# Key weights' low halves on VectorE, the first norm's spread one hook later, and a third in-projection block issued in two halves in a long convolution's last quarter

## The chip, the cores and the metric

The kernel runs on one core of one Trainium2 chip. The metric is the device time of one execution in microseconds (us). The engines are named as the profile names them: PE is TensorE (matrix products), PEld its weight load, DVE is VectorE, ACT is ScalarE, POOL is GpSimd and SP is the engine that issues the DMAs.

## What is computed

Two consecutive layers of a diffusion backbone work on 512 latent tokens of width 1024, with 256 context tokens. Layer 0 mixes with multi-head latent attention, layer 1 with an order-2 Hyena mixer; a gated feed-forward network with a three-tap convolution follows each. The two places that matter here, cut from the reference:

```python
hx = modulate(rmsnorm(x, norm_mix_g[i]), sh1, sc1)      # before each mixer
kv = h @ w_dkv                                          # layer 0, keys and values

def hyena_mixer(u, w_in, b_in, ...):                    # layer 1
    z = dwconv3(u @ w_in + b_in, conv_w, conv_b)
    x1, x2, v = jnp.split(z, 3, axis=-1)
    h_fwd, h_bwd = hyena_filters(...)
    v = v * x2
    y = (two_sided_fftconv(v, h_fwd, h_bwd) + v * d_bias) * x1
    return y @ w_out + b_out
```

`rmsnorm` needs the reciprocal root of the mean square of each token. `two_sided_fftconv` is a convolution over all 512 tokens, done in the kernel by matrix products with DFT tables.

## The kernel before

**Precision.** Nearly every matrix product is made of three: each operand is split into a high half (a rounded copy) and a low half (the rest), and `mm3` issues high x high, high x low and low x high into one accumulator. The names end in h and l: `wh`, `wl` are a weight tile's halves, made by `split_w` (lines 152 to 162) from the loaded `wr`: ScalarE casts `wh` (L158), and VectorE, or whichever engine is passed as `sub`, subtracts to get `wl` (L159), in columns of 1024.

**The start.** `filter_phase` computes the Hyena filters' spectra (`fps`, `fa`, `fb`, `fo` on TensorE; `fev` L503/504 and `fs` L514 on VectorE, stored to DRAM). In its gaps it calls `between()`, which each time runs the next entry of a list, the hooks: modulation rows, the squares of the first norm, then `nm.roots` (the reciprocal roots by three Newton rounds of L336 to L338, tile `rsq` of 128x128), then `spread`. `spread` calls `nm.finish`: VectorE writes `sqd` (L353), and TensorE's product with a matrix of ones, `bc`, spreads the roots over the partitions. Behind it, two hooks add the squares of the context (`add_ctx`: ScalarE squares at L312, GpSimd adds at L314, the last square is VectorE's at L319). Hooks HK (6) and 7 also load and split the key weights `wdkv0` (2048 columns) and `wdkv1` (1024 columns), with `sub` on GpSimd. Then `latents` forms the modulated input on VectorE and ScalarE (`hx` L365, `hxh` L366, `hxl` L367), and `kv` is its first product.

**The long convolution.** `hyena` works in four quarters of 256 channels, each a generator, `quarter(qi)`. A quarter projects three blocks of 256 columns: block 0 and 1 (`in_gemm`, accumulators `hz`) give the factors whose product is `u`; block 2 gives the gate `x1`, needed only at the very end of the quarter. `conv(b)` applies the three taps (L376 to L378, then the edge columns L1119/L1120). `turn` transposes u (`pt` on TensorE) into `uh`, `ul`. The forward DFT (`ua`, `ub`) follows, and the spectrum's steps: `se` (ScalarE) and `eo` (VectorE), then for each of two `kt`: sums `s`, products with the filter `fq` (`m`: half on VectorE, half on GpSimd), `zs`, `se`, and the split into `zzeh`, `zzel`, `zzoh`, `zzol` (cast on ScalarE at L1225, difference on VectorE at L1226). The inverse DFT, `py`, uses them; `yf` (L1239) is py times the gate. The quarters are interleaved by the loop at the end of `hyena`: while one quarter projects, the one before it finishes. In the last quarter nothing follows but the output projection (`project`, accumulators `pj`, weights `wout`), which needs `yh` and `yl`, the halves of yf. `split_y(range(6))` makes the first six chunks (ScalarE L1245, VectorE L1246), `split_y(range(6, 8))` the last two. yh and yl lie in the same memory as hh and hl, the input of the in-projection.

**What sets the order.** The program is written as one stream of calls; a scheduler lays it out into one queue for each engine, and an instruction may move ahead of others that it does not depend on. Each queue then runs strictly in its order. TensorE's accumulators, and the tiles with one or two buffers, tie the engines together.

Of the kernel before, what the change touches and what calls it, by code (L numbers as in the profile page):

```python
# [17 lines left out]
P = 128  # L18
# [8 lines left out]
HK = 6  # L27
# [31 lines left out]
def hybrid_kernel(ctx, tc, A, out):  # L59
    nc = tc.nc  # L60
# [463 lines left out]
    def mla():  # L524
        L = {}
        with ExitStack() as st:
            a1 = st.enter_context(tc.tile_pool(name="a1", bufs=1, side="left"))
            x = a1.tile([P, NC, T], F32, tag="x", name="x")
            xc = a1.tile([P, NC, TC], F32, tag="xc", name="xc")
            s2 = pick[1] = a1.tile([P, 8, 32], F32, name="s2")  # L530
            nc.gpsimd.memset(s2, 0.0)
            act(out=s2[:, :, 0], in_=V("c"), func=AF.Silu)
            act(out=s2[:, :, 1], in_=V("cctx"), func=AF.Silu)
            nc.gpsimd.tensor_copy(out=sc, in_=s2[:, :, 0])
            make_pick(a1)
            psum_pool(st, "pa", 5)
            mods = Mods([(0, 0, 2), (0, 2, 2)])

            slots = [(wp, "wh", 2), (wp, "wh", 2), (wp, "wl", 2), (wp, "wl", 2), (a1, "mw", 2), (a1, "mw", 2),
                     (wp, "wr", 3), (wp, "wr", 3)]  # L540
            ws = []

            def early():
                ws.extend(mods.load(mods.todo[k], *slots[k]) for k in range(NE))

            def ahead():
                ws.extend(mods.load(mods.todo[k], a1, "mw", 2) for k in range(2))

            def first_loads():
                ws.extend(mods.load(mods.todo[k], *slots[k]) for k in range(NE, 4))  # L550
                for i in range(4):
                    dma(out=x[:, 2 * i:2 * i + 2, :], in_=A["x"][:, 2 * i:2 * i + 2, :])
                ws.extend(mods.load(mods.todo[k], *slots[k]) for k in range(4, 8))
                dma(out=xc, in_=A["ctx"])

            nm = Norm(NC, 4, D, a1)
            nm_ctx = []
            hooks, started, wk = [], [], []
            L["wdkv"] = wk

            def between():
                if not started:
                    started.append(True)
                    first_loads()
                    step = lambda: mods.step_pe(1, ws, a1)
                    add = lambda j: (lambda: nm.add(x[:, j, :]))

                    def add_ctx(j0):
                        if not j0:
                            nm_ctx.append(Norm(NC, 2, D, a1))  # L570
                        for j in range(j0, j0 + 4):
                            nm_ctx[0].add(xc[:, j, :])

                    hooks.extend([()] * 2 + [(step, add(0), add(1))] + [(step, add(j)) for j in range(2, 8)] + [(step, ahead)])
                    hooks.append((lambda: L.update(yx=nm.roots(0, None, lane["last"])),))

                    def spread():
                        L["bcx"] = pso("bc")
                        nm.finish([L["bcx"]], 0, None, lane["last"], L["yx"])

                    hooks.append((spread,))
                    hooks.extend((lambda j=j: add_ctx(j),) for j in (0, 4))
                    hooks[HK] += (lambda: wk.append(split_w(A["wdkv0"], 2048, nc.gpsimd.tensor_tensor)),)
                    hooks[7] += (lambda: wk.append(split_w(A["wdkv1"], 1024, nc.gpsimd.tensor_tensor)),)
                elif hooks:
                    for f in hooks.pop(0):
                        f()

            filter_phase(early, between, mods)
            while hooks:  # L590
                between()
            at = atx.enter_context(tc.tile_pool(name="at", bufs=1, side="right", reuse_waits="tile"))
            L["at"] = at
            L["cos"] = at.tile([P, T], F32, name="cosq")
            L["sin"] = at.tile([P, T], F32, name="sinq")
            L["ckh"] = at.tile([P, 2, TK], F32R, name="ckh")
            L["ckl"] = at.tile([P, 2, TK], F32R, name="ckl")
            L["kb"] = [(at.tile([P, TK], F32R, name=f"kh{i}"), at.tile([P, TK], F32R, name=f"kl{i}")) for i in range(2)]
            dma(out=L["cos"], in_=A["rope"][0])
            dma(out=L["sin"], in_=A["rope"][1])  # L600
            with tc.tile_pool(name="a2", bufs=1, side="left", reuse_waits="tile") as a2:
                latents(lambda n: mods.step_pe(n, ws, a1, 2), nm, nm_ctx[0], a1, a1, a2, x, xc, L)
        with ExitStack() as st:
            ab = st.enter_context(tc.tile_pool(name="ab", bufs=1, side="left", reuse_waits="tile"))
            psum_pool(st, "pb", 7, 1)
            return attention(ab, L)
# [497 lines left out]
    def hyena(hh, hl):  # L1104
        with tc.tile_pool(name="hy", bufs=1, side="left", reuse_waits="tile") as hy:
# [17 lines left out]
            def quarter(qi):  # L1123
# [5 lines left out]
                x1 = []  # L1129
                pss = {}  # L1130

                def in_gemm(bs, parts):
# [5 lines left out]
                        jobs += [(pss[b][0], *w, 0), (pss[b][1], *w, P)]  # L1138
                    gemm(jobs, lambda k: hh[:, k, :], lambda k: hl[:, k, :], 8, parts)

                us = {}
                dv = lambda t: t.rearrange("p (n two) -> p two n", two=2)
                dv4 = lambda t: t.rearrange("p (n four) -> p four n", four=4)
# [28 lines left out]
                conv(1)  # L1172
                yield
                turn(0)
                in_gemm((2,), (slice(None),))
                conv(2)
                turn(1)
                yield
                if not M:
# [9 lines left out]
                for o in range(2):  # L1189
                    pa, pb = two((pst if o else pso)("ua")), two((pst if o else pso)("ub"))  # L1190
                    for i, ps in enumerate((pa, pb)):
                        for ci in range(2):
                            mm3(ps[:, ci], M[o][0][:, 2 * i + ci, :], M[o][1][:, 2 * i + ci, :], uh[:, 2 * i + o, :],
                                ul[:, 2 * i + o, :], True, True)
                    e = hy.tile([P, 2, 256], F32, tag="se", name="se", bufs=1)
                    nc.scalar.copy(out=e, in_=pa)
                    s0 = hy.tile([P, 2, 256], F32, tag=f"eo0{o}", name="eo0", bufs=1)
                    s1 = hy.tile([P, 2, 256], F32, tag=f"eo1{o}", name="eo1", bufs=1)
                    vtt(out=s0, in0=e, in1=pb, op=ALU.add)
                    if o:  # L1200
                        for ci in range(2):
                            vtt(out=s1[:, 1 - ci], in0=e[:, ci], in1=pb[:, ci], op=ALU.subtract)
                    else:
                        vtt(out=s1[:, 0], in0=e[:, 0], in1=pb[:, 0], op=ALU.subtract)
                        vtt(out=s1[:, 1], in0=pb[:, 1], in1=e[:, 1], op=ALU.subtract)
                    eo.append((s0, s1))
                for kt in range(2):
                    zs = []
                    for si, op in enumerate((ALU.add, ALU.subtract)):
                        s = eo[1][kt] if si else hy.tile([P, 2, 256], F32, tag="s0", name="s0", bufs=1)  # L1210
                        vtt(out=s, in0=eo[0][kt], in1=eo[1][kt], op=op)  # L1211
                        f = fq[:, kt, si]
                        m1 = hy.tile([P, 2, 256], F32, tag="m1", name="m1", bufs=1)
                        vtt(out=m1, in0=s, in1=f, op=ALU.mult)  # L1214
                        z = hy.tile([P, 2, 256], F32, tag=f"zs{si}", name=f"zs{si}", bufs=1)
                        vtt(out=z[:, 0], in0=m1[:, 0], in1=m1[:, 1], op=ALU.subtract)
                        m2 = hy.tile([P, 2, 256], F32, tag="m2", name="m2", bufs=1)
                        nc.gpsimd.tensor_tensor(out=m2[:, 0], in0=s[:, 0], in1=f[:, 1], op=ALU.mult)  # L1218
                        nc.gpsimd.tensor_tensor(out=m2[:, 1], in0=s[:, 1], in1=f[:, 0], op=ALU.mult)
                        nc.gpsimd.tensor_tensor(out=z[:, 1], in0=m2[:, 0], in1=m2[:, 1], op=ALU.add)  # L1220
                        zs.append(z)
                    for nm, op in (("e", ALU.add), ("o", ALU.subtract)):
                        s = hy.tile([P, 2, 256], F32, tag="s0", name="se", bufs=1) if nm == "e" else zs[1]
                        vtt(out=s, in0=zs[0], in1=zs[1], op=op)
                        nc.scalar.copy(out=zz[nm + "h"][:, kt], in_=s)  # L1225
                        vtt(out=zz[nm + "l"][:, kt], in0=s, in1=zz[nm + "h"][:, kt], op=ALU.subtract)  # L1226
# [210 lines left out]
```

## Time and profile before

| | |
|---|---|
| median of 3 runs | 1436.95 us (1435.52 to 1437.35) |
| profiled execution | 1438.24 us |
| its span | 1436.5 us |
| mean granted TensorE clock | 0.987 of full speed |
| PE busy | 1368.1 us (95%) |
| DVE busy | 965.6 us (67%) |
| ACT busy | 563.8 us (39%) |
| POOL busy | 238.9 us (17%) |

The profile is of one execution. Its span is the time from the first to the last instruction; the execution's own time is 1.7 us longer. Times in the rows below are from the span's start. A busy share is an average over stages that are limited by different things, so the rows below are read stage by stage.

### The profile page before, as it was taken

How to read it: one execution, taken by the hardware profiler on the slowest of the kernel's cores; microseconds unless marked ns; L12 is line 12 of the kernel's file. 1: busy time of each engine (PE TensorE's matmuls, PEld its weight loads, DVE VectorE, ACT ScalarE, POOL GpSimd, SP SyncE). 2: the span in 40 equal slices, each digit the busy share in tenths (PEclk: the TensorE clock that was granted, in tenths of full speed). 3: DMA queues.
4: the chain of work that ended last, by engine and by line, in shares of the span. 5: the costliest groups of instructions: out<-in, count | busy, mean ns of one | idle time of the engine just before them, and what ended most of it. 6: DMA issues, size and time to landing. Idle time of an engine off the chain costs nothing. (4 is left out here: it accounts for less than half of the span.)

```text
span 1436.5 us, 17449 instructions
## 1 busy us (share of the span) xinstructions
PE 1368.1 (95%) x6774; PEld 1073.1 (75%) x6774; DVE 965.6 (67%) x1473; ACT 563.8 (39%) x859; POOL 238.9 (17%) x216
## 2 busy tenths in 40 slices
PE   6789899999999999999999999999999999999996
PEld 3467666665589788787878988787788888888886
DVE  5766767677359777567764788988786553455545
ACT  5434455556335343134442443232344431234330
POOL 4701046456220000000001011332300000000011
PEclk9999999999999999999999999999999999999998
DMA  9663522224233645655514342222313213322121
GB/s 365 241 236 123 142 70 79 73 78 166 71 129 123 229 160 200 245 204 178 183 61 143 123 162 89 92 85 89 121 62 112 93 68 119 117 89 79 61 81 59
DMA packets 47966, 186.58 MB, mean 130 GB/s; under 512 B 5464, under 2 KB 18136, under 8 KB 33676
## 3 DMA queue, kind: packets, MB, share of 16 engines
q1 hardware_dynamic: 47884, 185.48, 37.2%
q8 instruction: 53, 0.87, 0.2%
q14 instruction: 29, 0.24, 0.1%
HBM read 171.29 MB, written 11.60 MB: 127 GB/s over the span
## 5 line engine op out<-in xcount | busy, mean ns | idle before, releaser
L158 ACT CAST wh<-wr 128x1024 fp32r<-128x1024 f32 (+1 forms) x203 | 190.2, 958 | 181.0 <-PE dn L69 89.3
L159 DVE TENSOR_TENSOR wl<-wr,wh 128x1024 fp32r<-128x1024 f32 x200 | 233.4, 1183 | 12.2 <-ACT wh L158 9.5
L314 POOL TENSOR_TENSOR sqa<-sqa,sq 128x512 f32<-128x512 f32 (+1 forms) x42 | 51.6, 1229 | 830.7 <-ACT sq L312 775.4
L69 PE MATMUL dn<-gh,wl 128*128 128x512 f32 (+1 forms) x396 | 147.0, 371 | 0.0
L69 PE MATMUL dn<-gh,wh 128*128 128x512 f32 (+1 forms) x396 | 146.6, 371 | 0.0
L69 PE MATMUL dn<-gl,wh 128*128 128x512 f32 (+1 forms) x396 | 146.6, 370 | 0.0
L377 DVE SCALAR_TENSOR_TENSOR z<-ua,vec,z 128x511 f32<-128x511 f32 x44 | 33.0, 749 | 107.1 <-ACT z L376 107.1
L1096 DVE SCALAR_TENSOR_TENSOR x<-dn,modc,x 128x512 f32<-128x512 f32 (+1 forms) x36 | 24.9, 691 | 108.8 <-PE dn L69 108.8
L376 ACT ACTIVATE z<-ua,vec 128x512 f32<-128x512 f32 x44 | 34.2, 778 | 146.2 <-PE ua L69 146.2
L69 PEld LDWEIGHTS dn<-gh,wh 128*128 128x128 f32 x396 | 74.5, 188 | 15.8 <-ACT wh L158 0.8
L850 POOL TENSOR_TENSOR acc<-acc,pf 128x512 f32<-128x512 f32 x60 | 81.2, 1378 | 24.1 <-ACT pf L840 23.5
L69 PEld LDWEIGHTS dn<-gh,wl 128*128 128x128 f32 x396 | 74.5, 188 | 14.1
L69 PEld LDWEIGHTS dn<-gl,wh 128*128 128x128 f32 x396 | 74.5, 188 | 13.8
L69 PE MATMUL hz<-hyh,wh 128*128 128x512 f32 (+1 forms) x224 | 82.3, 367 | 0.0
L69 PE MATMUL hz<-hyl,wh 128*128 128x512 f32 (+1 forms) x224 | 82.0, 367 | 0.0
L69 PE MATMUL hz<-hyh,wl 128*128 128x512 f32 (+1 forms) x224 | 81.5, 365 | 0.0
L840 ACT ACTIVATE pf<-s 128x512 f32<-128x512 f32 x96 | 57.2, 597 | 47.7 <-PE s L69 45.0
L69 PE MATMUL ua<-hf1h,wh 128*128 128x512 f32 (+1 forms) x192 | 72.8, 379 | 1.2 <-ACT hf1h L366 1.2
L69 PE MATMUL ua<-hf0l,wh 128*128 128x512 f32 (+1 forms) x192 | 72.4, 377 | 0.6 <-DVE hf0l L367 0.6
L69 PE MATMUL ua<-hf1l,wh 128*128 128x512 f32 (+1 forms) x192 | 72.6, 378 | 0.0
L69 PE MATMUL ua<-hf1h,wl 128*128 128x512 f32 (+1 forms) x192 | 72.5, 378 | 0.0
L69 PE MATMUL ug<-hf1l,wh 128*128 128x512 f32 (+1 forms) x192 | 72.5, 377 | 0.0
(394 smaller groups left out, 3392.4 us busy)
## 6 DMA issues: line engine op xcount, KB each, us to landing
wr<-in_wup SPq DMA_DIRECT2D x44, 1024.0 KB, 4.9
mw<-in_modw SPq DMA_DIRECT2D x40, 1024.0 KB, 5.4
wr<-in_wdn SPq DMA_DIRECT2D x32, 704.0 KB, 4.0
wr<-in_win SPq DMA_DIRECT2D x12, 1024.0 KB, 4.9
fspec<-fs SPq DMA_DIRECT2D x16, 256.0 KB, 4.0
mw<-in_modw SPq DMA_DIRECT2D x16, 256.0 KB, 2.7
wr<-in_wo SPq DMA_DIRECT2D x4, 1024.0 KB, 4.7
mw<-in_modw SPq DMA_DIRECT2D x8, 512.0 KB, 4.3
```

Source lines behind the costliest of these rows:

```text
L69: i = nc.tensor.matmul(*args, **kw)
L158: nc.scalar.copy(out=wh[:, c], in_=wr[:, c])
L159: sub(out=wl[:, c], in0=wr[:, c], in1=wh[:, c], op=ALU.subtract)
L314: nc.gpsimd.tensor_tensor(out=acc, in0=acc, in1=sq, op=ALU.add)
L376: act(out=z, in_=p, func=AF.Identity, bias=b, scale=w1)
L377: stt(out=z[:, 1:T], in0=p[:, 0:T - 1], scalar=w0, in1=z[:, 1:T], op0=ALU.mult, op1=ALU.add)
L840: act(out=pf, in_=s, func=AF.Exp, scale=ATT_SCALE)
L850: add(out=accs[h], in0=prev, in1=pf, op=ALU.add)
L1096: i = stt(out=x[:, q, c], in0=job[0][:, c], scalar=mcol(l, 5, q), in1=x[:, q, c], op0=ALU.mult, op1=ALU.add)
```

## The change

There are two independent parts.

First, at the start: `split_w` of both key weights no longer gets GpSimd's subtraction, so the three `wl` instructions (128x1024 each) go to VectorE. An empty hook is put in ahead of `spread`, so that spread and the two hooks of the context's squares come one call of `between()` later.

Second, in the last quarter (qi = 3): the third block's projection is no longer one group of 48 matrix products over both halves. A new helper, `gate_half(i, w)`, projects 128 columns (24 products) and applies their three taps. Half 0 is issued where the block stood, ahead of `turn(1)`; half 1 behind the forward DFT's loop and ahead of the loop over `kt`.

```diff
--- before.py
+++ after.py
@@ -578,10 +578,10 @@
                         L["bcx"] = pso("bc")
                         nm.finish([L["bcx"]], 0, None, lane["last"], L["yx"])
 
-                    hooks.append((spread,))
+                    hooks.extend([(), (spread,)])
                     hooks.extend((lambda j=j: add_ctx(j),) for j in (0, 4))
-                    hooks[HK] += (lambda: wk.append(split_w(A["wdkv0"], 2048, nc.gpsimd.tensor_tensor)),)
-                    hooks[7] += (lambda: wk.append(split_w(A["wdkv1"], 1024, nc.gpsimd.tensor_tensor)),)
+                    hooks[HK] += (lambda: wk.append(split_w(A["wdkv0"], 2048)),)
+                    hooks[7] += (lambda: wk.append(split_w(A["wdkv1"], 1024)),)
                 elif hooks:
                     for f in hooks.pop(0):
                         f()
@@ -1138,6 +1138,11 @@
                         jobs += [(pss[b][0], *w, 0), (pss[b][1], *w, P)]
                     gemm(jobs, lambda k: hh[:, k, :], lambda k: hl[:, k, :], 8, parts)
 
+                def gate_half(i, w):
+                    ps = pst(f"hz{i}")
+                    gemm([(ps, *w, i * P)], lambda k: hh[:, k, :], lambda k: hl[:, k, :], 8)
+                    x1.append(zconv(ps, 2 * qi + i, "x1", 4))
+
                 us = {}
                 dv = lambda t: t.rearrange("p (n two) -> p two n", two=2)
                 dv4 = lambda t: t.rearrange("p (n four) -> p four n", four=4)
@@ -1172,8 +1177,13 @@
                 conv(1)
                 yield
                 turn(0)
-                in_gemm((2,), (slice(None),))
-                conv(2)
+                if qi < 3:
+                    in_gemm((2,), (slice(None),))
+                    conv(2)
+                else:
+                    w2 = split_w(A["win"][3 * qi + 2], 2048)
+                    w2 = (wcols(w2[0], 8, 256), wcols(w2[1], 8, 256))
+                    gate_half(0, w2)
                 turn(1)
                 yield
                 if not M:
@@ -1204,6 +1214,8 @@
                         vtt(out=s1[:, 0], in0=e[:, 0], in1=pb[:, 0], op=ALU.subtract)
                         vtt(out=s1[:, 1], in0=pb[:, 1], in1=e[:, 1], op=ALU.subtract)
                     eo.append((s0, s1))
+                if qi == 3:
+                    gate_half(1, w2)
                 for kt in range(2):
                     zs = []
                     for si, op in enumerate((ALU.add, ALU.subtract)):
```

How the queues differ, at three places. On VectorE near the start, before (`rsq` are the root steps, `fs` and `fev` the filters'):

```order
L338 SCALAR_TENSOR_TENSOR rsq<-rsq 128x128
L514 SCALAR_TENSOR_TENSOR fs<-fo,fev 128x512
L336 SCALAR_TENSOR_TENSOR rsq<-rsq 128x128
L514 SCALAR_TENSOR_TENSOR fs<-fo,fev 128x512
L337 TENSOR_TENSOR rsq<-rsq 128x128
L514 SCALAR_TENSOR_TENSOR fs<-fo,fev 128x512
L338 SCALAR_TENSOR_TENSOR rsq<-rsq 128x128
L514 SCALAR_TENSOR_TENSOR fs<-fo,fev 128x512
L353 TENSOR_TENSOR sqd<-rsq,pick 128x512
L503 SCALAR_TENSOR_TENSOR fev<-fb,fee 128x512
```

and after:

```order
L338 SCALAR_TENSOR_TENSOR rsq<-rsq 128x128
L514 SCALAR_TENSOR_TENSOR fs<-fo,fev 128x512
L159 TENSOR_TENSOR wl<-wr,wh 128x1024 x2
L336 SCALAR_TENSOR_TENSOR rsq<-rsq 128x128
L514 SCALAR_TENSOR_TENSOR fs<-fo,fev 128x512
L337 TENSOR_TENSOR rsq<-rsq 128x128
L514 SCALAR_TENSOR_TENSOR fs<-fo,fev 128x512
L338 SCALAR_TENSOR_TENSOR rsq<-rsq 128x128
L159 TENSOR_TENSOR wl<-wr,wh 128x1024
L353 TENSOR_TENSOR sqd<-rsq,pick 128x512
L514 SCALAR_TENSOR_TENSOR fs<-fo,fev 128x512
L503 SCALAR_TENSOR_TENSOR fev<-fb,fee 128x512
```

Three `wl` came in ahead of `sqd`, and one `fs` went behind it.

On TensorE in the last quarter, where the first `py` of `kt` 0 stands, before (`hz` is the in-projection, `pj` the output projection; 52 `pj` stand ahead of this `py`):

```order
L69 MATMUL pj_8414<-yh,wh 128x512
L69 MATMUL pj_8414<-yl,wh 128x512
L69 MATMUL py<-ceh,zzeh 128x256
L69 MATMUL py<-cel,zzeh 128x256
L69 MATMUL py<-ceh,zzeh 128x256
L69 MATMUL py<-cel,zzeh 128x256
L69 MATMUL pj_8414<-yh,wl 128x512
L69 MATMUL py<-ceh,zzel 128x256
L69 MATMUL py<-seh,zzeh 128x256
```

and after:

```order
L69 MATMUL hz_8166<-hyl,wh 128x512
L69 MATMUL hz_8166<-hyh,wl 128x512
L69 MATMUL py<-ceh,zzeh 128x256
L69 MATMUL py<-cel,zzeh 128x256
L69 MATMUL py<-ceh,zzeh 128x256
L69 MATMUL py<-cel,zzeh 128x256
L69 MATMUL pj_8347<-yh,wh 128x512
L69 MATMUL pj_8348<-yh,wh 128x512
L69 MATMUL pj_8414<-yh,wh 128x512
L69 MATMUL pj_8415<-yh,wh 128x512
L69 MATMUL py<-ceh,zzel 128x256
```

The second half's 24 `hz` now stand right ahead of `py`, and all `pj` behind its first four.

On ScalarE there, before (`x` is the gate's first tap, `se` the spectrum's copies):

```order
L376 ACTIVATE x_8112<-hz_8057,hcc,vec 128x512
L1162 CAST uh<-pt 128x4x128
L1245 CAST yh<-yf 128x512 x5
L158 CAST wh<-wr 128x1024
L1196 COPY se<-ua 128x512
L1245 CAST yh<-yf 128x512
L1196 COPY se<-ua 128x512
L1225 CAST zzeh<-se 128x512
L1225 CAST zzoh<-zs_8210 128x512
L1225 CAST zzeh<-se 128x512
L1225 CAST zzoh<-zs_8236 128x512
```

and after:

```order
L1206 COPY se<-ua 128x512 x2
L158 CAST wh<-wr 128x1024
L376 ACTIVATE x_8191<-hz_8166,hcc,vec 128x512
L1237 CAST zzeh<-se 128x512
L1257 CAST yh<-yf 128x512 x6
L1237 CAST zzoh<-zs_8210 128x512
L158 CAST wh<-wr 128x1024
L1237 CAST zzeh<-se 128x512
L1237 CAST zzoh<-zs_8236 128x512
L1257 CAST yh<-yf 128x512 x2
```

The six `yh` went from ahead of the spectrum's copies to behind the first `zzeh`. VectorE's six `yl` follow them: before they stood among the steps of `kt` 0, now among those of `kt` 1.

## Rows read from the trace of the kernel before

**Rows 1.** Waits of TensorE, whole run: waited for: us in total, times, longest

```profile
PE bc L69 <- DVE sqd L353: 8.8, 3, 5.0
...
PE py L69 <- ACT zzeh L1225: 4.1, 2, 3.0
```

**Rows 2.** Timeline of VectorE at the start: start, length, instruction [idle before <-releaser]

```profile
58.25 1.89 DVE L338 SCALAR_TENSOR_TENSOR rsq<-rsq 128x128 f32<-128x128 f32 x1
...
63.07 1.82 DVE L337 TENSOR_TENSOR rsq<-rsq 128x128 f32<-128x128 f32 x1
...
65.42 0.28 DVE L338 SCALAR_TENSOR_TENSOR rsq<-rsq 128x128 f32<-128x128 f32 x1
...
66.22 0.68 DVE L353 TENSOR_TENSOR sqd<-rsq,pick 128x512 f32<-128x512 f32 x1
...
72.74 0.43 DVE L319 TENSOR_TENSOR sq<-xc 128x256 f32<-128x256 f32 x1 [3.45 <-POOL sqa L314]
```

**Rows 3.** Timeline of GpSimd at the start

```profile
57.53 7.21 POOL L159 TENSOR_TENSOR wl<-wr,wh 128x1024 fp32r<-128x1024 f32 x3
67.53 0.72 POOL L314 TENSOR_TENSOR sqa<-sqa,sq 128x256 f32<-128x256 f32 x1 [2.79 <-issue]
```

**Rows 4.** Timeline of ScalarE at the start

```profile
66.99 0.42 ACT L312 ACTIVATE sq<-xc 128x256 f32<-128x256 f32 x1 [6.41 <-DVE sqd L353]
```

**Rows 5.** Timeline of TensorE, the first ten steps of kv

```profile
75.83 0.80 PE L69 MATMUL kv<-hxh,wh 128*128 128x512 f32 x1 [4.26 <-ACT hxh L366]
...
80.62 0.46 PE L69 MATMUL kv<-hxl,wh 128*128 128x512 f32 x1
```

**Rows 6.** Timeline of TensorE in the long convolution's last quarter

```profile
969.68 0.48 PE L69 MATMUL hz<-hyh,wh 128*128 128x512 f32 x1
...
980.97 0.60 PE L1159 MATMUL pt<-cst,u 128*128 128x128 f32 x4
...
984.28 0.28 PE L69 MATMUL ua<-uh,dft1h 128*128 128x256 f32 x1
...
997.41 0.50 PE L69 MATMUL pj<-yl,wh 128*128 128x512 f32 x1 [1.19 <-DVE yl L1246]
...
1002.02 0.39 PE L69 MATMUL py<-ceh,zzeh 128*128 128x256 f32 x1 [1.07 <-ACT zzeh L1225]
...
1011.66 0.39 PE L69 MATMUL py<-ceh,zzeh 128*128 128x256 f32 x1 [3.03 <-ACT zzeh L1225]
...
1017.82 0.63 PE L69 MATMUL pj<-yh,wh 128*128 128x512 f32 x2
...
1023.54 0.39 PE L69 MATMUL pj<-yh,wh 128*128 128x512 f32 x1
```

**Rows 7.** Windows: us, busy (count) of PE, PEld, DVE, ACT, POOL, PEclk, DMA, GB/s

```profile
77.00:82.00 5.00, 5.00 (x15) 3.90 (x15) 4.74 (x8) 2.60 (x4) 0.00 (x0) 0.63 1.01 318
1012.00:1016.00 4.00, 4.00 (x22) 3.92 (x21) 1.03 (x2) 0.40 (x1) 0.00 (x0) 0.57 0.02 4
```

**Rows 8.** Timeline of VectorE in the quarters 2 and 3

```profile
943.20 0.69 DVE L1199 TENSOR_TENSOR eo<-se,ub 128x512 f32<-128x512 f32 x1 [0.27 <-PE ub L69]
...
966.40 1.22 DVE L159 TENSOR_TENSOR wl<-wr,wh 128x1024 fp32r<-128x1024 f32 x1
...
976.77 1.07 DVE L1153 TENSOR_TENSOR u<-z,zv 128x512 f32<-128x512 f32 x1
...
996.15 1.21 DVE L1246 TENSOR_TENSOR yl<-yf,yh 128x512 fp32r<-128x512 f32 x1
```

**Rows 9.** Timeline of ScalarE in the quarters 2 and 3

```profile
954.18 0.62 ACT L1225 CAST zzeh<-se 128x512 fp32r<-128x512 f32 x1 [8.93 <-DVE se L1224]
...
983.22 2.71 ACT L1245 CAST yh<-yf 128x512 fp32r<-128x512 f32 x5
```

## The prediction

> **What bounds the kernel now.** I read the waits of TensorE first, then the timelines of the two places that the change touches. TensorE carries the whole kernel; its waits are few and short, and two of the larger ones lie exactly where the change works [rows 1]. At the start TensorE stands 5.0 us until VectorE's `sqd` (the spread of the first norm's reciprocal roots) is done, and the stretch up to the first `kv` matmul at 75.83 is a chain across the engines. In the long convolution `py` waits twice for ScalarE's `zzeh`, 4.1 us in all. Both places end in TensorE work that nothing else can do, so what the chain there gains or loses is time of the whole kernel. Everything between and behind keeps its order, and I carry a shift at these places through to the end one for one.
>
> **Part A, the start.** On VectorE the root steps (`rsq`, 128x128) alternate with `fs` steps. Two of three consecutive rsq steps take 1.89 and 1.82 us (the one between them is of the same size), the last 0.28 [rows 2]. GpSimd runs its three `wl` exactly from 57.53 to 64.74 [rows 3]; the short step comes after that. So the long steps are VectorE waiting out a GpSimd instruction. From 58.25 to the start of sqd at 66.22 lie four pairs of one rsq and one fs. The last pair, behind GpSimd's end, takes 66.22 - 65.42 = 0.80 us. Four such pairs are 3.20 instead of 7.97: **-4.77**.
>
> Added on VectorE are three `wl` ahead of sqd. The same instruction on VectorE takes 1.22 us, of which the next one overlaps some 0.07 [rows 8]; 3 x 1.17 = **+3.5**. One fs goes behind sqd. Its size is that of sqd, 0.68 with 0.08 overlapped: **-0.6**. sqd therefore ends about 1.9 us earlier, at 65.0 instead of 66.9. GpSimd loses 7.2 us of work that is no one else's bound.
>
> Behind sqd stand the squares of the context, a relay between ScalarE and GpSimd: ScalarE's square waits for sqd (66.99), GpSimd's add starts at 67.53 and takes 0.72 [rows 3, 4], and VectorE's last square waits for the fifth add, at 72.74 [rows 2], 5.84 after the end of sqd (66.22 + 0.68). In the changed kernel four of the first five squares share one buffer, so that a square waits for the add before it: one turn is 67.53 - 66.99 + 0.72 + about 0.05 for the hand-over = 1.31, and five adds end some 6.15 after sqd: **+0.3**. So hx, hxh and the first kv matmul come 1.6 earlier, near 74.2. **A = -1.6.** No load stands before it: the weights' DMAs are issued at the hooks where they were issued, and SP's queue keeps its order there.
>
> Bounds for A: should the three wl run as slowly on VectorE as an rsq does now, they cost 1.8 each, 5.4 together, and A is +0.3; I do not take it, since GpSimd has nothing left to do beside them, and the wl of the row is nearer. In the other direction, the kv matmuls run 75.83 to 80.62 in ten steps of 0.48 us instead of 0.235 [rows 5], and the granted clock of 77 to 82 is 0.63 [rows 7]: 2.4 us are lost there to the lower clock of 1.2 GHz after the idle time before. If TensorE idles 1.6 less, a part of these may come back, up to -2.1 more. I take none of it, because the idle time behind sqd (from bc to hxh, 4.26) stays as it is. A lies between +0.3 and -3.7.
>
> **Part B, the last quarter.** Now 48 `hz` matmuls (3rd block, both halves) run from 969.68 to 980.97, then `pt`, 24 `py` of quarter 2 and the 24 matmuls of the DFT from 984.28 on [rows 6]. After the change 24 of the hz stand there and 24 behind the DFT. The TensorE work is equal; what counts is what it waits for.
>
> (1) 24 hz end at 969.68 + 5.65 = 975.33. `pt` (transposes) reads `u`, which VectorE writes from 976.77 to 977.84 [rows 8]; hz used to cover that. It is next in TensorE's order, and the py behind it are ready but stand behind it: **a hole of 2.5 us**. This wait is new.
>
> (2) pt and py take 984.28 - 980.97 = 3.3, of which a py (128x256) has 0.12 and the four pt the rest; the DFT has the size of py, 24 x 0.12 = 2.9. It ends at 984.1. The second half's 24 hz follow, to 989.7. Then `py` needs `zzeh`. Its chain starts at the first `eo`, 983.05 in the changed kernel, where the first half of the DFT is done (981.2 + 12 x 0.12 = 982.6) and ScalarE has copied it. In quarter 2, where no yl stands in this chain as none does after the change, it takes 954.18 + 0.62 - 943.20 = 11.6 us from eo to the end of zzeh [rows 8, 9]. So zzeh is there at 994.7: **a hole of 5.0 us**. Before, 52 `pj` (the projection that follows) covered this chain, and it only left 1.07 [rows 6]. They cannot come forward now: yh and yl lie in the space of hh and hl, which the last hz reads until 989.7, and ScalarE has its six `yh` behind zzeh in its queue.
>
> (3) The pj need yl. VectorE's six `yl`, which ran before in the chain of kt 0 beside the 52 pj (the last at 996.15), now stand between the steps of the second kt chain, behind wl and the shifted convolution, each 1.21 us beside GpSimd [rows 8]. From the order on VectorE and the durations of the rows: zzel at 996.4 (TensorE waits 0.25), yl0 at 999.05 (1.6), yl1 at about 1004 (2.1), yl2 (0.6), zzeh of kt 1 at 1008.5 (0.4). These come to **5.0 us**.
>
> (4) On the other side the old holes go: 1.07, 1.19 and 3.03 us before py, pj and py [rows 6], and with the last of them the low clock: from 1011.66 to 1017.82 TensorE runs 36 py and one pj, 6.16 us for what takes 36 x 0.12 + 0.34 = 4.66 at full clock; the granted clock of 1012 to 1016 is 0.57 [rows 7]. That is 1.5 us.
>
> Walked through: the second py group ends at 1013.7, and 62 pj of 0.233 (48 hz of the same size take 11.29) end at 1028.1. Before, the same point (the next pj behind them) is 1023.54 [rows 6]. **B = +4.6.** Lower bound: if GpSimd's six steps in the chain take the 0.72 of an undisturbed one [rows 3] instead of 1.0, zzeh is 1.6 earlier, B = +3.0. Upper bound: the clock may fall once more where nothing hides it, +1.5 by (4), and the yl may hold up GpSimd, +1.0; B = +7.1. A lower clock right after the 5.0 us hole costs nothing, because TensorE waits for yl there anyway.
>
> The upper bound has a rule beside it. The rows show that VectorE and GpSimd slow each other: an rsq of 0.28 takes 1.89 while GpSimd works [rows 2, 3]. The Trainium skill (SBUF - State Buffer, "SBUF: two separate sides") says that a VectorE instruction with two SBUF inputs and a GpSimd instruction that reads SBUF exclude each other for the whole instruction, whoever starts first. By it the six yl, now among GpSimd's steps of kt 1, would be added to them rather than overlap, and se of kt 1 came at 1008.2 instead of 1007.2: B = +5.6 instead of +4.6. For part A the rule and the rows say the same.
>
> **Sum.** -1.6 + 4.6 = +3.0 us. The profiled execution took 1438.24 (span 1436.5), 1.3 above the median of the three runs, 1436.95; the same difference on the median gives **1440.0**.
>
> **The rivals.**
> - Not slower (the other side): the kv clock. Price: up to 2.1 of the 2.4 us. If sqd 1.9 earlier shortens TensorE's idle time enough for the lower clock to end sooner, A = -3.7 and the sum +0.9: 1437.9, which is no change. It decides from 0.2 us of that loss upward. For it: the idle time before kv does get shorter. Against it: 4.26 of it stays. To the same end leads B at its lower bound, +1.4: 1438.4. Chance of both 0.25.
> - The second half fills the old holes. The 24 hz stand between the DFT and py, where TensorE used to wait; if zzeh came before they end (6.7 after the first eo) and pj had its yh by then, the 5.3 us of old holes and the 1.5 of clock were saved and only the hole at pt stayed: 2.5 - 5.3 - 1.5 = -4.3, with A -5.9: 1431. Against it: the 11.6 of quarter 2 and the order of ScalarE, yh behind zzeh. Chance 0.06.
> - The hole at pt or the yl cost more: the lower clock falls on py and the DFT (+1.5), and GpSimd is held up (+1.0). Sum +4.5 to +5.5: 1441.5 to 1442.5. For it: before, a hole of 3.03 was enough for a lower clock. Chance 0.25.
> - Part A does not do what it says: the rsq steps are slow for another reason than GpSimd. Then nothing comes off, VectorE has 3.5 more and 0.6 less to do, and the sum is 3.5 - 0.6 + 0.3 + 4.6 = +7.8: 1444.8. Against it: the steps are long exactly while GpSimd runs. Chance 0.04.
>
> **How the numbers follow.** The forecast, +3.0, has 0.40; its own range is 1439 to 1441.3. 0.2% is 2.9 us, about what a measurement of this kernel can tell from no change, and so the forecast lies on that line: half of it counts as slower, half as the same. Slower: 0.20 + 0.25 + 0.04 and a little for mixed cases = 0.50. Same: 0.20 + 0.22 = 0.42. Faster: 0.06 and the corner in which A and B both stand at their best (-3.7 + 3.0, with more) = 0.08. The range goes from 1437.0, where A's clock gain meets a B a little under the middle, to 1442.5, the rival with both extra costs. It leaves out 1431, 1444.8 and the corners.
>
> **What would show it.** In the changed profile: rsq steps of 0.3 to 0.8 us throughout, sqd ending near 65.0, the first kv near 74.2 (A; with the clock of the kv stretch still below 1). All later stamps are then about 1.6 earlier. In the last quarter: a hole of 2.5 before pt waiting for u; one near 5 before the first py of kt 0 waiting for zzeh; waits for yl behind it where before was one; no stretch of low clock over the last 32 py. I am wrong if zzeh is ready when the second half's hz end, if u is written earlier than 7 us behind the first hz, or if the kv matmuls run at full clock.

## The result: slower by half a percent

The changed kernel takes 1445.43 us (median of 10 runs, 1439.85 to 1449.27); the kernel before, beside it, takes 1437.07 (10 runs, 1435.52 to 1440.74). The ratio is 1.0055 with a 95% interval of 1.0042 to 1.0068, that is 7.9 us slower (6.0 to 9.8; the two medians are 8.4 apart). The profiled execution took 1446.38, its span 1444.6, the mean granted clock 0.982. I had forecast 3.0 us slower, with 1442.5 as the upper end of the range: the direction held, the size did not.

The waits of TensorE in the changed kernel, whole run (waited for: us in total, times, longest), answer to [rows 1]:

```profile
PE py L69 <- ACT zzeh L1237: 8.2, 2, 4.9
PE bc L69 <- DVE sqd L353: 6.7, 3, 3.5
...
PE pt L1164 <- DVE u L1158: 3.5, 5, 2.4
```

The longest wait for `sqd` became shorter (5.0 to 3.5), the waits for `zzeh` doubled in total (4.1 to 8.2), and one of 2.4 us for `u` is new. At the start, VectorE in the changed kernel (start, length, instruction), against [rows 2]:

```profile
62.59 0.28 DVE L336 SCALAR_TENSOR_TENSOR rsq<-rsq 128x128 f32<-128x128 f32 x1
...
64.39 1.21 DVE L159 TENSOR_TENSOR wl<-wr,wh 128x1024 fp32r<-128x1024 f32 x1
65.53 0.68 DVE L353 TENSOR_TENSOR sqd<-rsq,pick 128x512 f32<-128x512 f32 x1
...
72.18 0.42 DVE L319 TENSOR_TENSOR sq<-xc 128x256 f32<-128x256 f32 x1 [2.98 <-POOL sqa L314]
```

The root steps take 0.28 instead of 1.8. At this place the execution was already 1.3 us later than that of before (the same `fa` matmul starts at 57.59 before and 58.88 after; in the other profiles it lies between 57.3 and 60.0, early and late with part A and without), so the stamps must be compared from a common point. From that `fa` to the first `kv` (75.83 before, [rows 5]) it is 16.39 us instead of 18.24. Three fixed points in the trace of before, on TensorE (`cols` is the first product of the norm behind the output projection):

```profile
57.59 0.40 PE L69 MATMUL fa<-pqh,dfteh 128*128 128x512 f32 x1
...
969.27 0.66 PE L1159 MATMUL pt<-cst,u 128*128 128x128 f32 x4 [0.26 <-DVE u L1153]
...
1042.59 0.32 PE L69 MATMUL cols<-sqa,ones 128*32 128x64 f32 x8 [0.62 <-POOL sqa L314]
```

TensorE in the changed kernel:

```profile
58.88 0.40 PE L69 MATMUL fa<-pqh,dfteh 128*128 128x512 f32 x1
...
66.27 2.07 PE L69 MATMUL bc<-sqd,full 128*128 128x512 f32 x2 [3.04 <-DVE sqd L353]
...
75.27 0.50 PE L69 MATMUL kv<-hxh,wh 128*128 128x512 f32 x1 [3.36 <-ACT hxh L366]
...
967.65 0.66 PE L1164 MATMUL pt<-cst,u 128*128 128x128 f32 x4 [0.26 <-DVE u L1158]
...
976.35 0.63 PE L1164 MATMUL pt<-cst,u 128*128 128x128 f32 x4 [2.44 <-DVE u L1158]
...
984.14 0.40 PE L69 MATMUL hz<-hyh,wh 128*128 128x512 f32 x1
...
994.81 0.58 PE L69 MATMUL py<-ceh,zzeh 128*128 128x256 f32 x1 [4.91 <-ACT zzeh L1237]
...
1009.81 0.38 PE L69 MATMUL py<-ceh,zzeh 128*128 128x256 f32 x1 [3.27 <-ACT zzeh L1237]
...
1016.39 0.40 PE L69 MATMUL pj<-yh,wl 128*128 128x512 f32 x1
...
1049.88 0.32 PE L69 MATMUL cols<-sqa,ones 128*32 128x64 f32 x8 [0.63 <-POOL sqa L314]
```

The rows from 967.65 on are the last quarter, against [rows 6]. From the first of the last quarter's two `pt` (that of `turn(0)`, 967.65) to the first `cols` it takes 82.23 us; before, from 969.27 to 1042.59, 73.32. So in these two executions part A gains 1.85 us and part B loses 8.9; the rest, to the 8.1 us between the two spans, lies outside these two stretches (+1.3 ahead of `fa`, -1.1 between them, +0.8 behind `cols`). Inside the stretch, the holes before the second `pt` (2.44) and before the first `py` (4.91) are those that I had walked out (2.5 and 5.0). But TensorE does not wait for any `yl`; it waits 3.27 us for the `zzeh` of `kt` 1 instead. VectorE and GpSimd show why:

```profile
997.82 0.68 DVE L1223 TENSOR_TENSOR s<-eo,eo 128x512 f32<-128x512 f32 x1
998.42 0.69 DVE L1258 TENSOR_TENSOR yl<-yf,yh 128x512 fp32r<-128x512 f32 x1
999.02 0.68 DVE L1238 TENSOR_TENSOR zzol<-zs,zzoh 128x512 fp32r<-128x512 f32 x1
999.62 0.68 DVE L1226 TENSOR_TENSOR m<-s,fq 128x512 f32<-128x512 f32 x1
...
1003.31 0.68 DVE L1258 TENSOR_TENSOR yl<-yf,yh 128x512 fp32r<-128x512 f32 x1
1008.41 0.69 DVE L1236 TENSOR_TENSOR se<-zs,zs 128x512 f32<-128x512 f32 x1 [4.42 <-POOL zs L1232]
```

```profile
998.63 5.95 POOL L1230 TENSOR_TENSOR m<-s,fq 128x256 f32<-128x256 f32 x1 [5.25 <-issue]
1004.55 0.73 POOL L1231 TENSOR_TENSOR m<-s,fq 128x256 f32<-128x256 f32 x1
```

VectorE runs eleven instructions from 997.82 to 1003.99 without a pause, each at its undisturbed 0.6 us (0.33 for the small ones). GpSimd's first product, started when `s` was done, ends only behind them: 5.95 us, where the next product of the same size, with VectorE idle, takes 0.73. Only then do GpSimd's other five steps run, and `se` waits 4.42 us for them. Two stretches of lower clock lie beside it (us, busy of PE, PEld, DVE, ACT, POOL, then the granted clock), against [rows 7]:

```profile
994.00:1001.00 7.00, 6.19 (x20) 5.45 (x21) 7.00 (x14) 5.31 (x9) 2.37 (x1) 0.51 0.00 1
1011.00:1015.00 4.00, 4.00 (x23) 4.00 (x22) 2.66 (x4) 0.02 (x1) 0.00 (x0) 0.57 0.20 29
```

### The profile page after: what moved, and what is told of

It reads as the page before. It is cut to its first block, busy times and chain, and to the rows that moved or that the text cites. A ratio compares the mean times of both kernels' runs of the same rounds, so it can differ in the third digit from the quotient of the medians.

```text
span 1444.6 us, 17444 instructions
## 1 busy us (share of the span) xinstructions
PE 1372.4 (95%) x6774; PEld 1076.4 (75%) x6774; DVE 958.0 (66%) x1476; ACT 564.0 (39%) x859; POOL 236.4 (16%) x213
## 5 line engine op out<-in xcount | busy, mean ns | idle before, releaser
L159 DVE TENSOR_TENSOR wl<-wr,wh 128x1024 fp32r<-128x1024 f32 (+1 forms) x203 | 235.1, 1174 | 10.5 <-ACT wh L158 7.8
```

Source lines behind the costliest of these rows:

```text
L159: sub(out=wl[:, c], in0=wr[:, c], in1=wh[:, c], op=ALU.subtract)
```

## The experiments

All ratios below are against the kernel before, run beside each kernel on the same chip, with 95% intervals; 0.0010 is 1.4 us. Where two changed kernels are compared with each other, their ratios are subtracted, and the intervals of both count. The stretch from that first pt to cols (the stretch, in short) is taken from each profile, which is one execution.

**Part A alone, and its two halves.** The edit of `e1_a_alone` is part A's hunk of the diff. `e11_wl_alone` has this of it:

```diff
-                    hooks[HK] += (lambda: wk.append(split_w(A["wdkv0"], 2048, nc.gpsimd.tensor_tensor)),)
-                    hooks[7] += (lambda: wk.append(split_w(A["wdkv1"], 1024, nc.gpsimd.tensor_tensor)),)
+                    hooks[HK] += (lambda: wk.append(split_w(A["wdkv0"], 2048)),)
+                    hooks[7] += (lambda: wk.append(split_w(A["wdkv1"], 1024)),)
```

and `e12_hook_alone` the other half:

```diff
-                    hooks.append((spread,))
+                    hooks.extend([(), (spread,)])
```

> The kernel before with part A alone (three wl on VectorE, spread one hook later). In the changed kernel's trace the rsq steps fell to 0.28 us and TensorE's wait for sqd from 5.0 to 3.0 us. Theory 1 (GpSimd slowed the rsq steps, the gain is carried to the end): 1.6 to 2.0 us faster than before, ratio 0.9986 to 0.9989. Rival (A gains nothing at the end, because a stretch of lower clock or a later wait gives it back): within 0.5 us of before. Rival 2 (A is part of the loss): slower by 1 us or more.

> The kernel before with the three wl of the key weights on VectorE, without the empty hook. VectorE's, ScalarE's and TensorE's orders at the start are those of the changed kernel. Theory (the gain of part A is all in the wl): TensorE's wait for sqd 3.0 us, the time as that of part A alone, 0.9977 to 0.999. Rival (the hook is needed for it): no gain.

> The kernel before with the empty hook ahead of spread alone. VectorE's order at the start is that of before. Theory (the hook moves nothing but buffers): TensorE's wait for sqd stays 5.0 us, GpSimd's wl stay at 7.2 us in all, the context's squares turn every 1.25 us on one buffer as in the changed kernel, and the time is 0 to 0.5 us above before. Rival (the hook carries the gain): 1.5 us faster.

Measured: e1 0.9977 (0.9966 to 0.9989), 3.3 us faster; e11 0.9989 (0.9974 to 1.0004); e12 0.9997 (0.9983 to 1.0010). In the traces the gain can be read without the scatter of whole runs. From the fa matmul of above to the first kv it is 16.40 in e1 and 16.39 in e11, as in the changed kernel, and 18.33 in e12 as before. TensorE's wait for sqd, in e11 and in e12:

```profile
65.89 1.70 PE L69 MATMUL bc<-sqd,full 128*128 128x512 f32 x2 [3.03 <-DVE sqd L353]
```

```profile
68.55 2.08 PE L69 MATMUL bc<-sqd,full 128*128 128x512 f32 x2 [4.98 <-DVE sqd L353]
```

So in the traces the whole gain, 1.9 us, is the three wl; e11's time alone cannot be told from no change. The hook moves nothing, not even the buffers: the context's squares turn every 0.81 us in e12 as before, and every 1.25 in e11. I had put that slower relay down to the hook; it belongs to the wl. e1 as timed gains more than the 1.9 us of its trace, but its interval (1.6 to 4.9 us) holds that value. My rival on the other side, that the lower clock over kv ends earlier with A, is not seen: from the first to the last kv it is 30.29 to 31.73 us in the profiles with A and just as much in those without.

**Part B alone, and its split without the move.** `e2_b_alone` is the changed kernel with part A undone. `e8_b_both_old_place` is e2 with both halves at the old place:

```diff
                     gate_half(0, w2)
+                    gate_half(1, w2)
...
-                if qi == 3:
-                    gate_half(1, w2)
```

> The kernel before with part B alone (the last quarter's third block in two halves). Theory 1 (the whole loss is B's): 9 to 10 us slower than before, ratio 1.006 to 1.007, and GpSimd's first product of kt 1 again takes several us. My prediction's own sum: 4.6 us slower. Rival (the loss needs both parts): under 3 us slower.

> The kernel before with the third block issued as two halves one after the other, both at the old place ahead of pt. TensorE's work and its place are unchanged, only the order inside the 48 hz differs. Theory (the loss is where the second half stands, not the split): within 1 us of before, 0.9993 to 1.0007, no hole before pt, GpSimd's products near 1.2 us. Rival (the split alone, by later yh and yl or by the taps' order, costs): 3 us or more slower.

Measured: e2 1.0046 (1.0028 to 1.0063), 6.6 us slower; e8 0.9996 (0.9987 to 1.0005). e2's own trace shows the stretch at 81.45, 8.1 longer than before, and the same long product of GpSimd:

```profile
996.58 5.95 POOL L1230 TENSOR_TENSOR m<-s,fq 128x256 f32<-128x256 f32 x1 [5.25 <-issue]
```

The 5.95 us come again to the hundredth, so they are no accident of one execution. e8's stretch is 71.41, as in e12 (71.43), whose last quarter is that of before. Issuing the block in two halves is free; what costs is where the second half stands.

**GpSimd out of the chain of kt 1.** `e3_after_kt1_on_dve`, on the changed kernel:

```diff
+                        mul = vtt if qi == 3 and kt else nc.gpsimd.tensor_tensor
-                        nc.gpsimd.tensor_tensor(out=m2[:, 0], in0=s[:, 0], in1=f[:, 1], op=ALU.mult)
-                        nc.gpsimd.tensor_tensor(out=m2[:, 1], in0=s[:, 1], in1=f[:, 0], op=ALU.mult)
-                        nc.gpsimd.tensor_tensor(out=z[:, 1], in0=m2[:, 0], in1=m2[:, 1], op=ALU.add)
+                        mul(out=m2[:, 0], in0=s[:, 0], in1=f[:, 1], op=ALU.mult)
+                        mul(out=m2[:, 1], in0=s[:, 1], in1=f[:, 0], op=ALU.mult)
+                        mul(out=z[:, 1], in0=m2[:, 0], in1=m2[:, 1], op=ALU.add)
```

> The changed kernel with the six product steps that GpSimd does in kt 1 of the last quarter on VectorE instead; everything computed as before. Theory 1 (in the changed kernel VectorE's unbroken train of yl and spectrum steps keeps GpSimd's first product waiting, 5.95 us in the trace, and zzeh of kt 1 comes 3 to 4 us late for it): TensorE's wait before py of kt 1 goes from 3.3 us to under 0.5, the second low-clock stretch over py goes, and the time is 4 to 5 us below the changed kernel, so some 4 us above before. Rival (the product waits for its data, the filter's load or a buffer, not for VectorE): VectorE waits there in its place, se of kt 1 is no earlier, and the time stays at 8 us above before. Rival (the loss is in the holes of 2.4 and 4.9 us alone): less than 1 us better.

Measured: 1.0022 (1.0010 to 1.0035), 3.2 us above before and so 4.7 below the changed kernel. TensorE in e3:

```profile
990.84 0.58 PE L69 MATMUL py<-ceh,zzeh 128*128 128x256 f32 x1 [4.89 <-ACT zzeh L1238]
...
1000.54 0.50 PE L69 MATMUL pj<-yl,wh 128*128 128x512 f32 x1 [1.50 <-DVE yl L1259]
...
1002.97 0.28 PE L69 MATMUL py<-ceh,zzeh 128*128 128x256 f32 x1
```

The py of kt 1 no longer waits for zzeh; 1.50 us for a yl stand ahead of it. Between the first py of kt 0 and that of kt 1 there are 12.13 us instead of 15.00, and the py behind it run at full clock, 5.01 instead of 6.58 us to the next pj. Those two are 4.4 us, but 26 instead of 31 pj stand between the two py, and the five others cost 1.2 us behind them: 3.3 us are won. e3's stretch, 77.46, is 4.8 below the changed kernel's; the other 1.5 us are a lower clock behind the second pt that this execution did not have, and that its edit does not touch. The timed 4.7 us may hold some of the same chance. That the product waited for its data falls: VectorE reads the same filter at 995.65 without a pause.

**The order on VectorE alone.** Two kernels with the same instructions on the same engines as the changed one; a dependency of order puts the yl behind `se` of kt 1 (`e7_after_yl_behind`) or behind the first `m` of kt 1 (`e9_yl_after_m`):

```diff
...
-                    vtt(out=yl[:, j, :], in0=yf[:, j, :], in1=yh[:, j, :], op=ALU.subtract)
+                    in_order(lane["se"], vtt(out=yl[:, j, :], in0=yf[:, j, :], in1=yh[:, j, :], op=ALU.subtract))
```

(The dots stand for the lines that keep `se` in `lane["se"]`. e9 has `lane["m"]`, the last m that was issued for `si` 0.)

> The changed kernel with VectorE's yl put behind se of kt 1 by an order dependency; the same instructions on the same engines. Then m follows s directly again on VectorE, as in kt 0. Theory (the yl between s and m make VectorE's train unbroken and keep GpSimd out): GpSimd's first product of kt 1 takes about 1.2 us instead of 5.95, se of kt 1 comes some 7 us after s instead of 10.6, and zzeh of kt 1 some 3 us earlier; but 30 of the pj that stood ahead of py now follow it, 7 us of work, so that the time is 2 to 5 us above the changed kernel. Rival (the long product has another cause: the filter's load, or the place in the program): it stays near 6 us.

> The changed kernel with VectorE's yl put behind the first m of kt 1 by an order dependency, so that m follows s directly; three yl stay between the later steps of the chain. Theory (a step that needs the result just ahead of it leaves VectorE a moment of idling in which GpSimd is let in, and from then on they take turns): GpSimd's first product of kt 1 takes 1.0 to 1.6 us although yl follow, se of kt 1 comes 7 to 9 us after s. Rival (any yl in the chain shuts GpSimd out until the train ends): a product of 3 us or more is still there. By the count of pj that move behind py, 14, the time is within 3 us of the changed kernel.

Measured: e7 1.0087 (1.0073 to 1.0100), e9 1.0094 (1.0072 to 1.0116). Both are slower than the changed kernel, e7 by 4.6 us as expected, and in both GpSimd is let in. GpSimd in e7 and in e9:

```profile
998.43 1.18 POOL L1230 TENSOR_TENSOR m<-s,fq 128x256 f32<-128x256 f32 x1 [5.25 <-issue]
```

```profile
1001.00 1.18 POOL L1232 TENSOR_TENSOR m<-s,fq 128x256 f32<-128x256 f32 x1 [5.25 <-issue]
1002.14 1.17 POOL L1233 TENSOR_TENSOR m<-s,fq 128x256 f32<-128x256 f32 x1
```

VectorE in e9 now waits GpSimd out at most of the steps behind m, the first of them here:

```profile
1000.18 0.69 DVE L1223 TENSOR_TENSOR s<-eo,eo 128x512 f32<-128x512 f32 x1
1000.91 0.69 DVE L1226 TENSOR_TENSOR m<-s,fq 128x512 f32<-128x512 f32 x1
1001.52 1.21 DVE L1240 TENSOR_TENSOR zzol<-zs,zzoh 128x512 fp32r<-128x512 f32 x1
```

From py of kt 0 to py of kt 1 it is 13.2 us in both, 1.8 less than in the changed kernel. But only 5 (e7) and 11 (e9) instead of 31 pj stand between the two, so that 26 and 20 more are left for behind, and TensorE stands 8.67 us (e7) or 3.56 (e9) before its first yl. For e9 I had expected the time within 3 us of the changed kernel; it is 5.6 above, with a long stretch at the lower clock (0.50 from 996 to 1016).

**GpSimd out of the last quarter altogether.** The same edit as in e3 with `qi == 3` for the condition: `e4_before_q3_on_dve` on the kernel before, `e5_a_q3_on_dve` on it with part A, `e10_after_q3_on_dve` on the changed kernel. `e6_a_all_on_dve` is e5 with all four quarters on VectorE.

> The kernel before with all twelve GpSimd product steps of the last quarter on VectorE. The chain from s to zzeh has GpSimd's six steps in it, 6 us a kt beside VectorE's own. Theory 1 (GpSimd and VectorE take turns at the memory, so that six steps on VectorE at 0.34 us cost 2 us and save more than that): TensorE's waits of 1.07 and 3.03 us before py and the low clock behind the second shrink, 2 to 5 us faster than before. Rival (VectorE becomes the bound of the chain, with yl in it): no change, within 1 us.

> The kernel before with part A and with the last quarter's twelve product steps on VectorE (e1 and e4 together). The two places are 900 us apart. Theory (their gains add): e1 gave 0.9977, e4 0.9956, together 0.993, some 9 us faster than before; by the shifts of the traces alone (1.9 and 4.3) 6 us, 0.996. Rival (the larger part of e1 and e4 was chance of the low-clock stretches): 4 us.

> The changed kernel with all twelve product steps of the last quarter on VectorE, kt 0 too. Theory (what is left of part B's loss are the hole before pt, 2.4, and that before the first py, 4.9, whose chain runs from eo to zzeh): the first stays at 2.4, the second falls by the 2 us that the chain gets shorter, to about 3, and the time is some 2 us below the changed kernel with kt 1 alone on VectorE (1.0022), so 1.0005 to 1.001, and 4 to 5 us above the run with part A and the same products. Rival (part B costs nothing once GpSimd is out of the chain): equal to that run, 0.996.

> As the run before it, with the product steps of all four quarters on VectorE. In quarters 0 to 2 TensorE hardly waits for the chain (the two waits for zzeh lie in quarter 3). Theory (only an exposed chain is worth anything): the same as the run before it within 1 us. Rival (VectorE is the bound of the earlier quarters): 2 to 4 us slower than it, with waits of pt for u above 0.3 us.

Measured: e4 0.9956 (0.9938 to 0.9973), 6.3 us faster than before (2 to 5 expected); e5 0.9959 (0.9945 to 0.9973); e10 1.0010 (0.9996 to 1.0024); e6 1.0026 (1.0015 to 1.0038). In e4 TensorE no longer waits for zzeh before py of kt 0, nor for yl, and before py of kt 1 it waits 2.71 instead of 3.03 us [rows 6]:

```profile
1005.02 0.39 PE L69 MATMUL py<-ceh,zzeh 128*128 128x256 f32 x1 [2.71 <-ACT zzeh L1226]
```

The stretch is 68.96 instead of 73.32: 4.4 us, of which 1.5 are a low clock that this execution did not have. Against e12, which did not have it either, it is 2.5 less; e5, which had it, is with 70.20 us 3.1 below before. So 2.5 to 3.1 us are shown for the products; the time of e4 gained more (3.9 to 8.9), and why stays open. e5 should have added part A's 1.9 us and does not by its time; its trace has A's 16.40 us at the start, and the two intervals leave room for the 1.9. Its ratio is the 0.996 that I had added from the traces, not the 0.993 of the two timed ratios. These two are faster than both kernels; e5 and e4 cannot be told apart. e10 with the same products and part B is 5.1 thousandths, 7 us, above e5 (4 to 5 expected): GpSimd or not, part B loses. Its hole before pt is 2.43 as in the changed kernel, but the first py of kt 0 no longer waits for zzeh; the pj around it wait for yh and yl:

```profile
976.54 0.63 PE L1164 MATMUL pt<-cst,u 128*128 128x128 f32 x4 [2.43 <-DVE u L1158]
...
992.18 1.19 PE L69 MATMUL pj<-yh,wh 128*128 128x512 f32 x4 [2.09 <-ACT yh L1258]
994.79 0.67 PE L69 MATMUL pj<-yl,wh 128*128 128x512 f32 x1 [1.42 <-DVE yl L1259]
```

e6 missed what I expected of it: it is 9.6 us above e5, not level with it. TensorE's order in the earlier quarters came out differently, and it waits there for VectorE, for wl (5.8 us in two waits) and up to 2.1 us for u, where e5 has no wait for wl and at most 0.3 for u:

```profile
PE hz L69 <- DVE wl L159: 5.8, 2, 2.9
```

Whether that is VectorE's load or the other order of TensorE, this run does not separate.

## Where the prediction held and where it failed

**Part A** was right in its mechanism and near in its size, -1.6 foretold: from fa to the first kv it is 16.37 to 16.40 us in the nine profiles that have the wl on VectorE and 18.24 to 18.35 in the five others, 1.84 to 1.98 less. sqd came 1.97 us earlier (1.9 foretold); the relay behind it cost 0.1, not 0.3.

**Part B, steps (1) and (2)** held to 0.2 us, the clock aside. The hole before pt is 2.44 (2.5); from the second half's first hz to the first py it is 10.67 (10.6); the hole before it 4.91 (5.0). The rival in which the second half fills the old holes did not come true. None of the three signs by which I would have been wrong appeared; but two things that I had said would be seen did not come, the waits for yl and a last group of py without a low clock. They are steps (3) and (4).

**Step (3) failed in its mechanism.** I let VectorE and GpSimd take turns, so that each yl and each step of kt 1 took 1.1 to 1.2 us, and had TensorE wait for yl. VectorE took no turns: it ran at full speed, yl came early, and GpSimd stood still for 5.2 us. From the first py of kt 0 to that of kt 1 I had 13.8 us; it is 15.0. That is 1.2 us of the 4.3 that were missing. e7 and e9 have the turns that I had assumed, and there it is 13.2. My 1.21 us for a yl beside GpSimd was one row; the only other yl that ran beside GpSimd in that quarter of before took 0.69, and it was GpSimd that waited (VectorE, then GpSimd):

```profile
992.37 0.69 DVE L1246 TENSOR_TENSOR yl<-yf,yh 128x512 fp32r<-128x512 f32 x1
```

```profile
992.59 1.07 POOL L1218 TENSOR_TENSOR m<-s,fq 128x256 f32<-128x256 f32 x1 [29.79 <-DVE s L1211]
```

The Trainium skill (SBUF - State Buffer, "SBUF: two separate sides") says that the engine that starts first holds the shared port for the whole instruction; I weighed it as +1.0 us. The trace agrees that the two exclude each other and goes further: one instruction was held off for the length of ten.

**Step (4) failed in the clock**, and this is the larger part. I booked the old stretch of lower clock behind kt 1 as gone, 1.5 us; it is back in the changed kernel (36 py and three pj in 6.58 us, where I had 5.2 and e3, without the long product, takes 5.01): 1.4 us. And the clock fell also behind the new hole before pt: from the second pt to the second half's hz it is 7.79 to 7.81 us in the changed kernel, e7, e9 and e10, where I had 6.3, and 6.31 and 6.30 in e2 and e3: 1.5 us. I had this as a rival (+1.5, chance 0.25) and had not seen that both could come at once. 1.2 + 1.4 + 1.5, and 0.2 from steps (1) and (2), are the 4.3: that is 8.9 instead of 4.6. The same two instructions in e2:

```profile
975.79 0.63 PE L1164 MATMUL pt<-cst,u 128*128 128x128 f32 x4 [2.43 <-DVE u L1158]
...
982.10 0.40 PE L69 MATMUL hz<-hyh,wh 128*128 128x512 f32 x1
```

The lower clock is not fixed by the code. Behind kt 1, with the same instructions and a wait of 3.03 or 3.04 us ahead of them, the 36 py and one pj took 6.15 or 6.16 us in the traces of before, e1 and e11, and 4.65 or 4.67 in e8 and e12. In e12 the granted clock of the same window as in [rows 7] is 1.00 instead of 0.57:

```profile
1012.00:1016.00 4.00, 4.00 (x33) 3.93 (x34) 1.97 (x3) 1.04 (x2) 0.00 (x0) 1.00 0.02 4
```

In e3 and e10, where no wait stands right before the py, they ran at full clock. So one profile can differ from another by 1.5 us at this place alone, and the changed kernel has two such places. Its runs spread by 9.4 us, those of before by 5.2; that the two places make this spread is not shown. My 1.5 us in step (4) were the price of one execution, and the 8.9 us are those of one execution too. The timed loss of e2, 6.6 us (4.0 to 9.1), holds both my 4.6 and the 8.1 of its trace.

## What to carry to other kernels

A block of matmuls that covers a chain on other engines is worth what it covers. Before moving half of it, look who waits at the old place (here pt for u) and what shares memory with its data at the new one (here yh with hh). Where GpSimd holds a step of an exposed chain and VectorE has other work ready, do not count on turns: try the step on VectorE where it is exposed (here 2.5 to 3.3 us in the traces); doing so in the other quarters too made this kernel 9.6 us slower, for a reason that stayed open. And read a change of 1 or 2 us from a stretch between two fixed instructions in the trace, several times over: the one at the start repeats to 0.03 us with part A, where whole runs scatter by several, but that over the unchanged last quarter lies between 71.43 and 73.35, by the clock for the most part.

## What the runs showed of the hardware that I had not expected

VectorE's unbroken train of instructions with two inputs in SBUF held a GpSimd instruction off for all of its length: 5.95 us for a 128x256 product that takes 0.73 alone, twice the same in two kernels. With only VectorE's order changed, so that m stands directly behind the s that it needs (the step from s to m is 0.73 instead of 0.60 us), the same product took 1.18 us, and the engines alternated. What decides in general when GpSimd is let in is open: in kt 0 of the kernel before a yl stands between s and m, VectorE has no pause there, GpSimd's product starts 0.2 us behind that yl as in the changed kernel, and GpSimd got in all the same (1.07 us). I did not try other gaps.
